# Two-layer hybrid encoder on one core: where a branch's gate products run, how they are kept, and when its decays are read

## The chip, the cores and the metric

The kernel runs on one core of one Trainium2 chip. The metric is device time in microseconds of one execution of the whole program, both layers and both sequences. The engines are TensorE (PE, its weight loads apart as PEld), VectorE (DVE), ScalarE (ACT), GpSimd (POOL) and SyncE (SP), which issues all DMAs of this kernel from one queue.

## The reference, cut to what matters

Two sequences of 256 and 512 tokens (T = 768 together) go through two layers with 1024 channels. `layer` below is one of them; the three branches are a state-space scan (SSD), gated linear attention (GLA) and attention, and each has a sigmoid gate.

```python
h = rmsnorm(x, norm1_w)
z, xbc, dt_raw, gq, gk, gv, gog, glr, aq, ak, av, gates = split(h @ w_in)
# SSD: xbc through a depthwise conv of 5 taps and silu, dt by softplus; chunks of 128 tokens
y = y_forward + y_backward + xs * d_skip
o_ssd = rmsnorm(y * silu(z), norm_w)
o_gla = gla(gq, gk, gv, gog, glr)      # forward and backward, chunks of 64 tokens
o_att = attention(aq, ak, av)
g = sigmoid(gates)                     # three gates of 1024 channels
merged = g[0] * (o_ssd @ w_br_ssd) + g[1] * (o_gla @ w_br_gla) + g[2] * (o_att @ w_br_attn)
x = x + merged @ w_out
x = x + (silu(gate) * up) @ w_ffn_out  # on rmsnorm(x, norm2_w), 2816 hidden channels
```

All inputs and outputs are float32.

## The kernel before

The activations lie transposed: 128 channels on the partitions, the 768 tokens along the free dimension. A float32 product is made from two float32r parts of each side, a rounded one and the rest ("hi" and "lo"): for a block of 128 output channels and 1024 input channels `gemm_a` issues 3 pairs of parts x 8 blocks of channels x 2 halves of the tokens = 48 matmuls of 128x384 into one PSUM tile of 768 columns. There are two such PSUM tiles (`pg`). The short products of the scans (128x256, 128x128, 128x64 columns) are plain float32. A product's weights come in units of four blocks (512 columns, 256 KB): `wunit` loads a unit into one of three raw tiles, ACT writes its rounded part and POOL (DVE in the stages where `lo_eng` is set so) the rest, into five pairs of tiles.

A layer is recorded in this order (`layer`, L782): norm; attention with the first inputs of the GLA between its blocks; `ssd_dt` (step sizes, cumulated decays and the decays' factors of the SSD); the GLA's other inputs (`gla_qk`, `gla_v`) and its output gate `gog`; the GLA, two pairs of heads one after the other, each forward and backward (`gla_pair`), followed by the eight products `g2` and `ba` of the attention's gate and its branch; the SSD in four groups (`ssd_inputs` with four `xbc` products each, `ssd_group`), between which the eight `g1` and `bg` products of the GLA's branch stand; then the loop of the SSD's gated outputs (L869: eight `z` products, silu, times y, split into parts, sum of squares), its norm, the eight `g0` and `bs` products of the SSD's branch; `wo`; and the feed-forward part.

Nothing runs in the recorded order. Every operation is first recorded in a plan; `schedule` then lets the plan run on assumed costs (`cost`; a DMA is taken to land 1900 ns behind its transfer) and hands each engine, whenever it is free, the operation with the lowest number whose inputs and buffers are there. What is recorded under `first` comes before everything else. So operations recorded later fill an engine while an earlier chain waits, if their buffers are free: tiles of one stage share SBUF cells with those of the next. The order so found is written out and fixed: each engine, and SP's queue, does its operations one by one, and waits for what the next one needs. All instructions therefore carry the line of `emit`, L563, and are told apart by their shapes and tiles (`base_S` and `base_P` are the kernel's lasting tiles in SBUF and PSUM, `cell` those of a stage, `wts` the weights, `d_...` tensors kept in DRAM).

Tiles that matter below: `ea` (two, used by every gate and every gated output), `ld` (one, into which y, partial sums and the residual are loaded), `yz` (eight pairs, the split outputs of the SSD).

## Time and profile before

| what | value |
|---|---|
| time, median of 3 runs | 3194.85 us (3192.27 to 3194.99) |
| the profiled execution | 3194.44 us, span 3192.7 us |
| mean granted TensorE clock | 0.98 |
| busy: PE, PEld, DVE, ACT, POOL | 96%, 94%, 50%, 40%, 29% |
| ACT table loads | 149 |
| HBM read, written | 235 MB, 41 MB |

The span is what lies between the first and the last instruction. A busy share is a mean over stages that differ: the feed-forward part (1060 to 1601 us in the first layer) is nothing but matmuls, the scans are chains through PE, DVE, ACT and POOL. The granted clock is 1.00 where TensorE runs at its upper level, 2.4 GHz, and 0.5 at the lower, 1.2 GHz; a mean between them tells what share of a stretch was at which.

### The profile page before, as it was taken

Reading aid. Unit: us, or ns where it says so; the run is one execution under the profiler, and the core shown is the slowest. Engines: PE = TensorE matmul, PEld = TensorE weight load, DVE = VectorE, ACT = ScalarE, POOL = GpSimd, SP = SyncE. Lnnn points to the kernel's source line nnn. Section 1 sums busy time; section 2 is a strip of 40 time slices with the busy share of each in tenths; the row PEclk is TensorE's granted clock in tenths of the full one; section 3 lists DMA queues with packets and bytes.
Section 4 is the critical chain, followed back from the end, with each engine's and each line's share of the span. In section 5 each row is a group of like instructions: output and inputs, shape, how many; then the busy total and the mean of one; then the engine's idle time right before and its main releaser. Section 6 shows DMA issues by size and latency. Waiting matters only on the chain.

```text
span 3192.7 us, 46598 instructions
## 1 busy us (share of the span) xinstructions
PE 3068.3 (96%) x18160; PEld 2997.0 (94%) x18160; DVE 1604.1 (50%) x2777; ACT 1262.3 (40%) x2153; POOL 932.1 (29%) x932
## 2 busy tenths in 40 slices
PE   8989988999999999999999899799999999999998
PEld 7989977899999999999999899599999999999998
DVE  4765578666423332333447556776663234333333
ACT  4667545444323221212346665444443232222123
POOL 4533544554232000000164244355533320000002
PEclk8999988999999999999999999799999999999999
DMA  3223213443334322222222232133443252222222
GB/s 109 60 74 111 92 43 100 124 118 107 98 88 132 115 62 65 62 65 61 90 78 65 74 118 81 38 110 116 117 126 90 86 178 64 63 63 64 63 60 70
DMA packets 191949, 279.31 MB, mean 87 GB/s; under 512 B 16688, under 2 KB 89776, under 8 KB 191728
## 3 DMA queue, kind: packets, MB, share of 16 engines
q1 hardware_dynamic: 191728, 276.32, 29.3%
q8 instruction: 143, 2.34, 0.3%
q14 instruction: 78, 0.64, 0.1%
HBM read 235.17 MB, written 41.09 MB: 87 GB/s over the span
## 4 chain that ended last, share of the span: by engine, by line
PE 86%; DVE 8%; DMA 3%; ACT 2%; issue 1%; POOL 0%; SPq 0%; DVEq 0%; POOLq 0%; ACTq 0%
PE base_P L563 86%; DVE cell L563 7%; DMA cell<-d_cs 2%; ACT cell L563 1%; DVE base_S L563 1%; DMA d_ce<-cell 1%; ACT L563 0%; ACT base_S L563 0%; DMA cell<-d_ce 0%; POOL cell L563 0%; SPq L563 0%; DMA base_S<-wts 0%; DMA cell<-xT 0%; DMA base_S<-d_part 0%; POOL base_S L563 0%
## 5 line engine op out<-in xcount | busy, mean ns | idle before, releaser
L563 PE MATMUL base_P<-base_S 128*128 128x384 f32 (+3 forms) x12452 | 2265.6, 335 | 42.9 <-DVE cell L563 21.2
L563 PEld LDWEIGHTS base_P<-base_S 128*128 128x128 f32 x12452 | 2113.8, 190 | 58.4 <-DVE cell L563 23.6
L563 ACT ACTIVATE base_S<-base_S 128x512 fp32r<-128x512 f32 (+6 forms) x830 | 550.6, 668 | 1299.2 <-PE base_P L563 914.2
L563 DVE TENSOR_TENSOR base_S<-base_S,base_S 128x512 fp32r<-128x512 f32 (+1 forms) x400 | 281.5, 704 | 692.1 <-issue 526.1
L563 PE MATMUL base_P<-cell,base_S 128*128 128x384 f32 x3136 | 574.2, 337 | 0.0
L563 POOL TENSOR_TENSOR cell<-cell,base_S 128x256 f32<-128x256 f32 (+3 forms) x164 | 183.9, 1132 | 1319.0 <-ACT base_S L563 1288.8
L563 PEld LDWEIGHTS base_P<-cell,base_S 128*128 128x128 f32 x3136 | 550.8, 188 | 0.0
L563 POOL TENSOR_TENSOR base_S<-base_S,base_S 128x512 fp32r<-128x512 f32 (+1 forms) x232 | 315.9, 1363 | 449.3 <-ACT base_S L563 192.0
L563 DVE TENSOR_TENSOR base_S<-base_P,base_S 128x768 f32<-128x768 f32 (+1 forms) x276 | 231.5, 839 | 295.5 <-PE base_P L563 284.0
L563 PE MATMUL base_P<-cell,cell 128*128 128x256 f32 (+3 forms) x1568 | 314.7, 325 | 21.8 <-DVE cell L563 16.4
L563 PEld LDWEIGHTS base_P<-cell,cell 128*128 128x128 f32 x1568 | 237.8, 191 | 50.7 <-DVE cell L563 19.4
L563 DVE TENSOR_TENSOR cell<-base_P,cell 64x128 f32<-64x128 f32 (+5 forms) x385 | 201.7, 528 | 155.7 <-PE base_P L563 93.6
L563 ACT ACTIVATE cell<-base_P 128x256 f32<-128x256 f32 (+5 forms) x344 | 148.3, 440 | 177.3 <-PE base_P L563 156.5
L563 POOL TENSOR_TENSOR cell<-cell,cell 128x256 f32<-128x256 f32 (+6 forms) x244 | 179.4, 747 | 95.8 <-DVE cell L563 59.1
L563 PE MATMUL base_P<-base_S,cell 128*128 128x128 f32 (+2 forms) x908 | 161.6, 288 | 39.9 <-ACT cell L563 19.0
L563 ACT ACT_TABLE_LOAD x149 | 191.2, 1283 | 7.9 <-DMA cell<-xT 5.3
L563 ACT ACTIVATE cell<-cell 128x768 f32<-128x768 f32 (+9 forms) x228 | 133.2, 608 | 128.4 <-DVE cell L563 122.0
L563 PEld LDWEIGHTS base_P<-base_S,cell 128*128 128x128 f32 x908 | 116.0, 156 | 63.2 <-ACT cell L563 22.8
L563 DVE SCALAR_TENSOR_TENSOR cell<-cell,base_S,cell 128x770 f32<-128x770 f32 x128 | 150.5, 1175 | 30.9 <-ACT cell L563 27.8
L563 DVE TENSOR_TENSOR cell<-cell,base_S 128x1024 f32<-128x1024 f32 (+3 forms) x85 | 87.4, 1050 | 32.0 <-DMA cell<-d_cs 22.6
L563 POOL TENSOR_TENSOR base_S<-base_S 128x768 f32<-128x768 f32 x32 | 67.0, 2095 | 110.1 <-DVE base_S L563 110.1
L563 DVE TENSOR_TENSOR cell<-base_P,base_S 128x256 f32<-128x256 f32 (+1 forms) x136 | 67.0, 512 | 63.1 <-PE base_P L563 61.2
(58 smaller groups left out, 1194.5 us busy)
## 6 DMA issues: line engine op xcount, KB each, us to landing
base_S<-wts SPq DMA_DIRECT2D x584, 256.0 KB, 2.6
cell<-d_cs SPq DMA_DIRECT2D x96, 256.0 KB, 4.7
d_part<-base_S SPq DMA_DIRECT2D x32, 384.0 KB, 2.8
base_S<-d_part SPq DMA_DIRECT2D x32, 384.0 KB, 3.5
base_S<-wts SPq DMA_DIRECT2D x32, 272.0 KB, 2.7
d_y<-cell SPq DMA_DIRECT2D x48, 128.0 KB, 3.7
base_S<-d_y SPq DMA_DIRECT2D x16, 384.0 KB, 3.4
d_x<-base_S SPq DMA_DIRECT2D x16, 384.0 KB, 2.5
```

What stands on the lines that cost most here:

```text
L563: f(*[real(x) for x in op.args], **{k: real(x) for k, x in op.kw.items()})
```

## The change

- The eight `z` products, with silu, are recorded behind `g2`/`ba` in the GLA's stage; the results go to DRAM (`d_z`), and the loop of gated outputs loads them.
- Six of the eight `g0` products, with sigmoid, are recorded earlier: two behind the SSD's last group, one behind every second gated output; the results go to DRAM (`d_g0`) and are loaded where `gate_branch` used to make them. `g0` 6 and 7 stay.
- The gates `g1` and `g2` are made by tanh, which shares a table with exp in the plan (`SETS`): sigmoid(x) is (1 + tanh(x/2))/2. The half is left to the end: the branch's product is multiplied by 2 for the SSD, and `wo`'s result by 0.5. These factors ride in SCALAR_TENSOR_TENSOR instructions that replace TENSOR_TENSOR ones.
- The tail of `ssd_dt`, which reads the chunk ends' decays back from DRAM (`ce`) and takes their exponentials, becomes `ssd_decays` and is recorded behind `gla_v(1)`.
- The plan's landing time of a DMA is 8400 ns with an element-strided side in SBUF, 4000 ns with a broadcast source, and 1900 ns else.

```diff
-SETS = {"Exp": (0,), "Ln": (5,), "Sigmoid": (2,), "Silu": (18,), "Sqrt": (3,)}
+SETS = {"Exp": (0,), "Tanh": (0,), "Ln": (5,), "Sigmoid": (2,), "Silu": (18,), "Sqrt": (3,)}
...
+    def landing(out, src):
+
+        if any(v.dims[-1][0] > 1 and v.dims[-1][1] not in (0, 1) and v.buf.space == "S" for v in (out, src)):
+            return 8400
+        if any(s == 0 and n > 1 for n, s in src.dims):
+            return 4000
+        return 1900
...
-                        op.end = start + cost + 1900
+                        op.end = start + cost + op.landing
...
         self.gla_v(1)
+        self.ssd_decays()
...
             self.gate_branch("g2", "ba", m, self.o_att, None, self.d_part[m])
+
+        early = [("z", m) for m in range(8)] + [("g0", m) for m in range(6)]
+        for _ in range(8):
+            self.early_gate(*early.pop(0))
...
+            for _ in range((0, 0, 0, 2)[g]):
+                self.early_gate(*early.pop(0))
...
-            ps = self.gemm_in(l, "z", m)
             ea = self.ev.tile([P, T], F32, tag="ea", bufs=2)
-            self.dve.tensor_tensor(out=ea, in0=ps, in1=self.r1, op=ALU.mult)
-            self.act.activation(ea, ea, AF.Silu)
+            self.sp.dma_start(ea, self.d_z[m])
...
+            if m % 2 and early:
+                self.early_gate(*early.pop(0))
+        for g in early:
+            self.early_gate(*g)
...
-            mg.append(self.gate_branch("g0", "bs", m, yz, self.d_part2[m], None, rs))
+            mg.append(self.gate_branch("g0", "bs", m, yz, self.d_part2[m], None, rs, self.d_g0[m] if m < 6 else None))
...
-            self.dve.tensor_tensor(out=x, in0=ps, in1=x, op=ALU.add)
+            self.dve.scalar_tensor_tensor(out=x, in0=ps, scalar=0.5, in1=x, op0=ALU.mult, op1=ALU.add)
...
+    def early_gate(self, name, m):
+        ps = self.gemm_in(self.l, name, m)
         with self.first():
             ea = self.ev.tile([P, T], F32, tag="ea", bufs=2)
             self.dve.tensor_tensor(out=ea, in0=ps, in1=self.r1, op=ALU.mult)
-            self.act.activation(ea, ea, AF.Sigmoid)
+            self.act.activation(ea, ea, AF.Silu if name == "z" else AF.Sigmoid)
+            self.sp.dma_start((self.d_z if name == "z" else self.d_g0)[m], ea)
...
+            if gate is None:
+                self.dve.tensor_tensor(out=ea, in0=ps, in1=self.r1, op=ALU.mult)
+            else:
+                self.sp.dma_start(ea, gate)
+
+            if rs is None:
+                self.act.activation(ea, ea, AF.Tanh, scale=0.5)
+            elif gate is None:
+                self.act.activation(ea, ea, AF.Sigmoid)
...
-            self.dve.tensor_tensor(out=ea, in0=ps2, in1=ea, op=ALU.mult)
+            if rs is None:
+                self.dve.scalar_tensor_tensor(out=ea, in0=ea, scalar=1.0, in1=ps2, op0=ALU.add, op1=ALU.mult)
+            else:
+                self.dve.scalar_tensor_tensor(out=ea, in0=ps2, scalar=2.0, in1=ea, op0=ALU.mult, op1=ALU.mult)
```

What that does to the engines' fixed order is shown at three places of the first layer. In the second layer they look alike. The emitting line is L563 before and L574 now, and the lasting tiles are numbered 83 to 85 before and 87 to 89 now.

**ACT, behind the attention's blocks.** `base_S<-cell 128x192` is the exponential of the chunk ends' decays, which needs `ce` from DRAM; the rows around it are the attention's and the weights' (`128x512`). Before:

```order
L563 ACTIVATE base_S_85<-cell_3_500 128x128
L563 ACTIVATE cell_3_287,cell_3_294<-base_P_84,cell_3_294 128x256
L563 ACTIVATE cell_3_530<-base_P_84 128x256
L563 ACTIVATE base_S_85<-base_S_83 128x512
L563 ACTIVATE base_S_83<-cell_3_550 128x192
L563 ACTIVATE cell_3_550<-base_P_84 64x256
L563 ACTIVATE cell_3_834<-base_P_84 128x512
```

Now:

```order
L574 ACTIVATE cell_3_554<-base_P_88 64x256
L574 ACTIVATE cell_3_507,cell_3_301<-base_P_88,cell_3_301 128x256
L574 ACTIVATE base_S_89<-base_S_87 128x512
L574 ACTIVATE base_S_87<-cell_3_554 128x192
L574 ACTIVATE cell_3_534<-base_P_88 128x256
L574 ACTIVATE base_S_89<-cell_3_1100 128x128
L574 ACTIVATE base_S_87<-base_S_87 128x192
```

The exponential moved 17 instructions back, behind the rows of the attention that used to follow it; on SP's queue the load of `ce` moved behind the next two loads of weights.

**DVE, in the GLA's second pair, backward direction.** Rows with `128x770` are the taps of the SSD's conv, those with `cell_5` tiles belong to the SSD, `base_S<-base_P,base_S 128x768` scales a gate's or output gate's product, `COPY_PREDICATED` and `64x...` rows are the GLA's. Before:

```order
L563 TENSOR_TENSOR cell_5_4027<-base_P_84,base_S_83 128x256
L563 TENSOR_TENSOR cell_5_4027<-base_P_84,base_S_83 128x512
L563 TENSOR_TENSOR cell_4_3089<-cell_4_3089,cell_4_2796 128x768
L563 COPY cell_4_2821<-cell_4_3089 64x6x64
L563 TENSOR_TENSOR cell_4_2863<-cell_4_2796,cell_4_2965 64x768 x2
L563 TENSOR_TENSOR cell_4_3101<-cell_4_3101,cell_4_2798 128x768
L563 SCALAR_TENSOR_TENSOR cell_5_4062<-cell_5_3634,base_S_83,cell_5_4062 128x770 x4
L563 TENSOR_TENSOR cell_5_3634<-base_P_84,base_S_83 128x256
L563 TENSOR_TENSOR cell_5_3634<-base_P_84,base_S_83 128x512
L563 COPY cell_4_2821<-cell_4_3089 64x6x64
L563 SCALAR_TENSOR_TENSOR cell_5_4116<-cell_5_3634,base_S_83,cell_5_4116 128x770 x2
L563 TENSOR_TENSOR cell_4_2821<-cell_4_2821,cell_4_2798 128x768
```

Now:

```order
L574 TENSOR_TENSOR base_S_87<-base_P_88,base_S_87 128x768
L574 SCALAR_TENSOR_TENSOR cell_4_3061<-base_S_87,cell_4_2829 128x64 x3
L574 TENSOR_TENSOR base_S_87<-cell_4_3061 128x6
L574 TENSOR_TENSOR cell_4_3091<-cell_4_3091,cell_4_2795 128x768
L574 TENSOR_TENSOR cell_4_2853<-cell_4_2795,cell_4_2975 64x768 x2
L574 TENSOR_TENSOR base_S_87<-base_P_88,base_S_87 128x768
L574 TENSOR_TENSOR cell_4_3112<-cell_4_3112,cell_4_2797 128x768
L574 COPY cell_4_2810<-cell_4_3091 64x6x64 x2
L574 TENSOR_TENSOR cell_4_2810<-cell_4_2810,cell_4_2797 128x768
```

The `xbc` products of the SSD's first group, which filled TensorE here with their convs behind them, have made room for the `z` products with one scaling each; `xbc` 0 to 3 now stand behind the GLA's last matmul.

**SP, at the loop of the SSD's gated outputs.** `d_y` and `d_z` are the outputs and their gates, `d_g_0` the SSD branch's gates, `wts` units of weights. Before, from the last store of the GLA's branch on:

```order
L563 DMA d_part_0_61<-base_S_83 128x768
L563 DMA base_S_83<-d_y_64 128x768
L563 DMA base_S_83<-wts 128x512 x2
L563 DMA base_S_83<-d_y_64 128x768
L563 DMA base_S_83<-wts 128x512 x2
```

Now, at the loop's end:

```order
L574 DMA base_S_87<-d_z_66 128x768 x2
L574 DMA base_S_87<-wts 128x512
L574 DMA base_S_87<-d_y_64 128x768
L574 DMA base_S_87<-wts 128x512
L574 DMA d_g_0_67<-base_S_87 128x768
L574 DMA base_S_87<-wts 128x512
L574 DMA base_S_87<-d_y_64 128x768
L574 DMA base_S_87<-d_z_66 128x768 x2
L574 DMA base_S_87<-d_y_64 128x768
L574 DMA d_g_0_67<-base_S_87 128x768
```

The loop no longer has a product between two loads of y: it has loads of its own for the gates, and the loads for its last two outputs stand behind units of weights, the last of them the second unit of `bs` 3. On TensorE the six `g0` products stand in one row behind the SSD, then `bs` 0 to 5, then `g0` 6.

## Rows read from the trace of the kernel before

**Rows 1.** The page: busy us, share of the span and instructions of each engine.

```profile
PE 3068.3 (96%) x18160; PEld 2997.0 (94%) x18160; DVE 1604.1 (50%) x2777; ACT 1262.3 (40%) x2153; POOL 932.1 (29%) x932
```

**Rows 2.** Stretches of both layers: length, busy us (x instructions) by engine, granted clock.

```profile
core 0: us, PE busy (x) PEld busy (x) DVE busy (x) ACT busy (x) POOL busy (x), PEclk, DMA share, GB/s
183.00:223.00 40.00, 28.41 (x193) 26.70 (x193) 22.69 (x68) 22.71 (x58) 13.53 (x15) 0.91 0.24 53
293.00:382.00 89.00, 88.52 (x504) 86.86 (x503) 45.01 (x80) 52.31 (x72) 51.15 (x47) 1.00 0.34 104
382.00:494.00 112.00, 90.98 (x467) 78.58 (x466) 80.88 (x176) 56.45 (x121) 44.91 (x62) 0.88 0.17 49
494.00:773.00 279.00, 264.27 (x1570) 253.24 (x1570) 202.40 (x304) 125.11 (x186) 156.13 (x155) 0.98 0.41 115
773.00:840.00 67.00, 67.00 (x385) 67.00 (x385) 35.45 (x38) 28.40 (x38) 13.91 (x7) 1.00 0.38 113
1755.00:1796.00 41.00, 29.00 (x193) 27.03 (x193) 23.21 (x70) 22.39 (x58) 13.44 (x15) 0.88 0.19 51
1955.00:2067.00 112.00, 91.25 (x469) 78.81 (x467) 80.12 (x176) 55.80 (x120) 45.20 (x61) 0.88 0.17 48
2067.00:2346.00 279.00, 265.03 (x1573) 254.02 (x1574) 203.33 (x305) 126.21 (x188) 157.83 (x154) 0.98 0.40 115
```

**Rows 3.** Waits from 183 to 223 us: total, times, longest us.

```profile
ACT base_S L563 <- DMA cell<-d_ce: 9.1, 1, 9.1
...
PE base_P L563 <- ACT cell L563: 8.4, 1, 8.4
...
PE base_P L563 <- DVE cell L563: 3.0, 2, 1.6
```

**Rows 4.** Timeline of SP, then of ACT: start us, us, instruction, idle before.

```profile
189.02 0.56 SPq L563 DMA_DIRECT2D d_ce<-cell  x1
189.68 1.00 SPq L563 DMA_DIRECT2D d_gv<-base_S  x2
197.76 0.32 SPq L563 DMA_DIRECT2D cell<-d_ce  x1
```

```profile
192.95 0.63 ACT L563 ACTIVATE base_S<-base_S 128x512 fp32r<-128x512 f32 x1
202.67 0.54 ACT L563 ACTIVATE base_S<-cell 128x192 f32<-128x192 f32 x1 [9.10 <-DMA cell<-d_ce]
203.24 1.00 ACT L563 ACTIVATE cell<-base_P 64x256 f32<-64x256 f32 x2
...
212.62 0.62 ACT L563 ACTIVATE base_S<-base_S 128x512 fp32r<-128x512 f32 x1
```

**Rows 5.** Groups of PE's matmuls from 382 to 494 us, by shape.

```profile
L563 PE MATMUL base_P<-base_S 128*128 128x384 f32 x251 | 51.6, 356 | 7.2 <-DVE cell L563 5.3 <-ACT base_S L563 1.9
```

**Rows 6.** Timeline of PE where the GLA ends and the SSD begins.

```profile
493.70 1.01 PE L563 MATMUL base_P<-base_S 128*128 128x384 f32 x2 [1.92 <-ACT base_S L563]
500.03 2.29 PE L563 MATMUL base_P<-base_S 128*128 128x384 f32 x6 [5.32 <-DVE cell L563]
```

**Rows 7.** DVE's groups: conv taps from 382 to 494 us; then z's stretch, 773 to 860; then the feed-forward part.

```profile
L563 DVE SCALAR_TENSOR_TENSOR cell<-cell,base_S,cell 128x770 f32<-128x770 f32 x10 | 11.7, 1169 | 3.3 <-ACT cell L563 3.2
```

```profile
L563 DVE TENSOR_TENSOR base_S<-base_S,base_S 128x512 fp32r<-128x512 f32 x20 | 17.9, 895 | 16.5 <-issue 8.9 <-PE base_P L563 7.6
L563 DVE TENSOR_TENSOR base_S<-base_P,base_S 128x768 f32<-128x768 f32 x10 | 9.6, 957 | 13.0 <-PE base_P L563 13.0
L563 DVE SCALAR_TENSOR_TENSOR cell<-base_S,cell 128x768 fp32r<-128x768 f32 x8 | 8.2, 1020 | 11.0 <-ACT cell L563 11.0
L563 DVE TENSOR_TENSOR base_S<-base_S 128x768 f32<-128x768 f32 x8 | 7.7, 959 | 3.1 <-ACT base_S L563 3.1
```

```profile
L563 DVE TENSOR_TENSOR base_S<-base_S,base_S 128x512 fp32r<-128x512 f32 x115 | 79.0, 687 | 214.2 <-issue 172.9 <-PE base_P L563 41.3
```

**Rows 8.** ACT's and POOL's groups in z's stretch, 773 to 860 us.

```profile
L563 ACT ACTIVATE base_S<-base_S 128x512 fp32r<-128x512 f32 x21 | 13.3, 632 | 42.9 <-PE base_P L563 35.1 <-issue 7.4 <-ACT base_S L563 0.4
L563 ACT ACTIVATE cell<-base_S 128x768 fp32r<-128x768 f32 x8 | 7.4, 925 | 0.0
```

```profile
L563 POOL TENSOR_TENSOR cell<-cell,base_S 128x768 f32<-128x768 f32 x7 | 13.6, 1949 | 57.1 <-ACT base_S L563 57.1
```

**Rows 9.** DMA issues from 773 to 1060 us: count, KB each, median us to landing.

```profile
base_S<-d_y SPq DMA_DIRECT2D x8, 384.0 KB, 3.5
...
cell<-d_x SPq DMA_DIRECT2D x8, 384.0 KB, 6.1
```

**Rows 10.** ACT's table loads in the whole program.

```profile
L563 ACT ACT_TABLE_LOAD x149 | 191.2, 1283 | 7.9 <-DMA cell<-xT 5.3
```

**Rows 11.** DVE's SCALAR_TENSOR_TENSOR out of PSUM, whole program.

```profile
L563 DVE SCALAR_TENSOR_TENSOR base_S<-base_P,base_S 128x768 f32<-128x768 f32 x4 | 3.8, 953 | 0.1
```

More of the change, by code (lines that the diff above doesn't have):

```diff
@@ L257 @@
     __slots__ = ("i", "eng", "fn", "args", "kw", "deps", "succ", "cost", "prio", "bufs", "wait", "ready", "end",
-                 "table", "label", "port")
+                 "table", "label", "port", "landing")
 class Proxy:
@@ L349, in record @@
         op.port = eng == "gpsimd" or eng == "vector" and all(v.buf.space == "S" for v in writes + reads)
+        if eng == "sync":
+            op.landing = self.landing(writes[0], reads[0])
         for j in deps:
@@ L380, in cost @@
         return 60 + nbytes / 340
+    @staticmethod
+    def landing(out, src):
[4 more added lines that the diff above has]
+        return 1900
     @staticmethod
@@ L795, in layer @@
         self.d_x = dram("d_x", [8, P, T])
+        self.d_z = dram("d_z", [8, P, T])
+        self.d_g0 = dram("d_g0", [8, P, T])
         self.d_x2 = dram("d_x2", [8, P, T])
@@ L991, in gate_inputs @@
         self.dve.tensor_tensor(out=self.glr[64:128], in0=dtg[64:128], in1=gh[64:128].bitcast(F32), op=ALU.subtract)
-    def gate_branch(self, gname, bname, m, acts, part_in, part_out, rs=None):
-        l = self.l
-        ps = self.gemm_in(l, gname, m)
+    def early_gate(self, name, m):
+        ps = self.gemm_in(self.l, name, m)
         with self.first():
@@ L998, in gate_branch @@
             self.dve.tensor_tensor(out=ea, in0=ps, in1=self.r1, op=ALU.mult)
-            self.act.activation(ea, ea, AF.Sigmoid)
+            self.act.activation(ea, ea, AF.Silu if name == "z" else AF.Sigmoid)
+            self.sp.dma_start((self.d_z if name == "z" else self.d_g0)[m], ea)
+    def gate_branch(self, gname, bname, m, acts, part_in, part_out, rs=None, gate=None):
+        l = self.l
+        ps = self.gemm_in(l, gname, m) if gate is None else None
+        with self.first():
+            ea = self.ev.tile([P, T], F32, tag="ea", bufs=2)
+            if gate is None:
[6 more added lines that the diff above has]
+                self.act.activation(ea, ea, AF.Sigmoid)
             if rs is not None:
@@ L1384, in ssd_dt, with ssd_decays @@
         self.csn = sn[:, :, 64:128].rearrange("p t (d x) -> p t d x", d=2)[:, :, :, 0:16]
+        self.ce = ce
+    def ssd_decays(self):
+        mp, ce = self.mp, self.ce
         self.ecs = self.cp.tile([P, NT, 2, 16], F32, tag="ecs")
```

## The prediction

> **What bounds the kernel now.** I read the page's shares first: PE 96% and PEld 94% of the span [rows 1]. The reader should see that only about 125 us of the span lie outside PE's busy time, and that no product is removed by this change: TensorE gets the same matmuls in another order. What can be won is idle time and time at the lower clock. So I read the stretches next, and count for each what it loses: its idle time plus (1 - granted clock) times its length. In layer 0, with layer 1 behind it [rows 2]:
>
> - attention's end, 183 to 223: 11.6 idle + 3.6 clock = 15.2 (layer 1: 12.0 + 4.9 = 16.9);
> - the GLA's first pair, 293 to 382: 0.5 idle, clock 1.00, nothing to win;
> - its second pair, 382 to 494: 21.0 + 13.4 = 34.4 (20.8 + 13.4 = 34.2);
> - the SSD, 494 to 773: 14.7 + 5.6 = 20.3 (14.0 + 5.6 = 19.6);
> - the `z` products, 773 to 840: 67.0 of 67.0 busy at 1.00, nothing lost, 385 matmuls, so 0.174 us each.
>
> Together 70 us a layer. The z products are thus a dense block that stands where nothing needs filling, and the change carries it to where 34 us are lost. The last two views are the waits and the timelines, which say why PE stands still: in the first stretch ACT waits 9.1 us for `d_ce`, and PE waits 8.4 us for ACT behind it [rows 3].
>
> **Term 1, the decays: +10 us a layer (4 to 12).** The store of `ce` is issued at 189.02, its load at 197.76, and ACT, idle from 193.6, reads it at 202.67 [rows 4]. All 17 rows which now stand ahead of that exponential ran behind it, from 203.24 to 213.24, so they are 10.0 us of work that ACT can start at 193.6. It reaches the exponential near 203.6, when the load, even if it is not issued earlier, has landed (ACT went on at 202.67). The load moved past two loads of weights on SP, each about a microsecond of queue; that eats the margin and no more. PE's 8.4 us behind ACT goes, and with it most of the clock's 3.6: 12.0. PE's 3.0 us behind DVE [rows 3] stays. I take 10. The low end, 4, is for PE finding half of the wait again at the next link of the attention's chain.
>
> **Term 2, the GLA's second pair: +27 (20 to 34).** PE ran 251 matmuls of 384 columns there, the `xbc` 0 to 3 and a part of `g1` [rows 5], by 0.174 us 43.7 us of filling. Its own work is then 112 - 34.4 - 43.7 = 33.9 us at the full clock. In their place come eight z products, 384 x 0.174 = 66.8 us: 33.9 + 66.8 = 100.7. If the GLA's chain keeps its 112 us, 11.3 are lost. It should be shorter: the ten conv taps of 1.169 us leave DVE for the later stage [rows 7], against eight scalings of about 0.957 that come [rows 7]; and the matmuls of the chain itself run at 1.00, not 0.88. With no idle gaps the loss is 0. I take 7: 34.4 - 7 = 27. The ends are 34 (no loss) and 20 (a loss of 14, the chain 3 us longer because ACT's silu and its tables stand in it).
>
> **Term 3, the SSD: +3 (-10 to +8).** The 251 displaced matmuls go here: 279 - 20.3 = 258.7 us of work become 302.4. The SSD's own chain fits in some 270, so PE has more to do than the chain is long, and the filling is there. The two gaps of 1.92 and 5.32 at the border [rows 6] are the first SSD matmuls waiting for convs; now `xbc` 0 to 3 stand densely behind the GLA, which wins these 7.2. But the head start is gone: group 0's convs, 10 taps by 1.169 [rows 7] among them, must run before its first short products, with only `g1` and `bg` as cover; if that gives 4 us back I am at +3. The low end, -10, is a whole conv of a group of 10 to 12 us uncovered; the high end 8 is the border gap with no cost.
>
> By PE's row the stage loses 20.3; the weight loads give another reading. The Trainium skill, "Trainium Kernel Development and Optimization", section "Performance Expectations", calls the busy time of matmuls a bad metric, since they are pipelined, and that of weight loads a good one. By it the stage is 253.2 of 279 busy [rows 2] and loses 25.8, and if that were won the sum would have 5.5 us a layer more (3119 rather than 3130, an estimate from that page's rule and these rows).
>
> **Term 4, the loop of gated outputs and the SSD's branch: -8 (-3 to -20).** The loop used to be covered by z's own 66.8 us. Now six `g0` products cover it: 6 x 48 x 0.174 = 50.1 us from the SSD's end. The loads for the last outputs stand behind units of weights in SP's one queue, the last behind the second unit of `bs` 3. That unit needs a raw tile and a pair of tiles for its parts, which come free only as `g0` 5's weights are released, at about 50.1. With hi, 0.63 [rows 8], and lo, 0.90 [rows 7], y6 is issued near 52 and lands 3.5 us later [rows 9], at 55.5. There is one `ld` tile, so y7 waits for y6's product of 0.96 [rows 7], and lands near 60. Each needs another 0.96, then hi 0.93 [rows 8] and lo 1.02 [rows 7]: the parts are there at 58.4 and 62.9. `bs` 0 starts at 50.1, reaches block 6 after 24 matmuls at 54.3 and waits 4.1; it reaches block 7 another 18 later, 61.5, and waits 1.4. `bs` 2 needs a PSUM tile, which waits for the norm's factor behind the last sum of squares (POOL's additions, 1.949 each [rows 8]): about 2 us. Sum 7.5, taken as 8. If y6 and y7 land earlier, 3 stay. With d_x's 6.1 us for a load [rows 9] in place of 3.5, twice, and a lower clock behind the gap, it is up to 20.
>
> On DVE beside POOL the row shows 895 ns for the weights' lo part in z's stretch, against 687 where DVE works alone in the feed-forward part [rows 7]. I use 895 for the lo part and the rows as they are for the others. The Trainium skill, "SBUF — State Buffer", section "SBUF: two separate sides", says that DVE and GpSimd share a port pair by an exclusive lock, so that a DVE operation with two SBUF inputs and a GpSimd operation that reads SBUF exclude each other for a whole instruction. The trace agrees in sign only: 208 ns more is far from a whole 1949. By that rule the last two steps would lose one POOL addition each, 3.9 us a layer, and the sum would be 3138.
>
> **Edits costed at nothing.** SCALAR_TENSOR_TENSOR out of PSUM takes 953 ns [rows 11], TENSOR_TENSOR 957 [rows 7]: no change. The tables go from 149 loads [rows 10] to 105 in the new order, 44 x 1.283 = 56 us of ACT; ACT is 40% busy [rows 1] and in the stages with gates PE waits for it seldom, so they win nothing beside PE, and cost nothing. Stores and loads of `d_z` and `d_g0` are 28 of 0.39 MB a layer, 11 MB, against a DMA share of 0.17 in the second pair's stretch and 0.41 in the SSD's [rows 2]; PE covers them. Without that cover, 28 landings of 3.5 us would be 98 us a layer.
>
> **Sum.** 10 + 27 + 3 - 8 = 32 us a layer, 64 in both. The profiled execution was 3194.44 with a span of 3192.7, and the median of the runs is 3194.85, 0.4 above, so it is a fair base: 3194.4 - 64 = 3130.
>
> **The rivals.**
>
> *A, the chains are the bound, not PE's filling.* The GLA's chain stays 112 us and takes silu's detours on ACT, and group 0's late start makes the SSD's chain the longest: term 1 is 10, term 2 20, term 3 -10, term 4 -8, so 12 a layer, 3170. For it: in the stretch of 382 to 494 PE waits 7.2 us for DVE and 1.9 for ACT only in the filling's own rows [rows 5], so the filling itself was late. Against it: the first pair, filled with products, has a clock of 1.00 and 88.5 of 89 busy [rows 2].
>
> *B, the SSD gains as well.* With 43.7 us more to choose from, its loss falls from 20.3 to about 5: term 3 is 15 and not 3, term 4 -4. (10 + 27 + 15 - 4) x 2 = 96, so 3098. For it: the stretch loses only 7% now. Against it: what remains idle there may be chains with nothing to overlap.
>
> *C, slower: the loop's tiles.* One `ld`, two `ea` tiles for stores and loads: eight gated outputs of 3.5 landing and about 3.7 of work (product, hi, lo and square: 7.2) and four uses for `g0` of about 4.8 (scaling, gate and a store of 2.9, an estimate from the load's 3.5) make (8 x 7.2 + 4 x 4.8)/2 = 38 us with two tiles, under g0's 50.1. It decides only if the loop's loss goes over 40 us a layer, that is if each use of a tile takes about 17 us. At 6.1 for each load [rows 9] it would be 11 us a layer more, not enough: 3152. Behind 40, slower than 3194.
>
> *D, DVE stands still for POOL's whole addition in the loop's last two steps*: 2 x 1.949 [rows 8] a layer, 3138, within the likeliest one's range; the 208 ns of [rows 7] speak for a small part of it only. It is what the rule of the Trainium skill's "SBUF — State Buffer", told above, would do.
>
> **How the numbers follow.** Likeliest, the four terms: 0.60 (of that 0.10 for D), own range 3105 to 3150. A: 0.20. B: 0.13. C, or that nothing changes: 0.07. The time of the likeliest is 3130. The range is 3092 to 3170: it takes in B and A with the bounds of their terms and leaves out C. A run can be told from no change at about 0.2%, 6 us: faster 0.93, within that 0.03, slower 0.04.
>
> **What would show it.** Term 1: no wait of ACT on `d_ce` in 183 to 223, PE's busy time near 28 in about 30 us. Term 2: 384 more z matmuls there, granted clock 0.95 or above from 382 on, where it was 0.88. Term 3: a stretch of about 300 us between the GLA's last matmul and the SSD's, with `xbc` 0 to 3 without a gap at its head. Term 4: a gap of PE at the first `bs`, behind `d_y` or DVE, of some 6 us, and y6's load issued only when `g0` 5 ends. ACT has 105 table loads. I am wrong if the clock stays below 0.9 in the second pair (A), if PE has gaps over 10 us behind the SSD's convs, or if the gap ahead of `bs` is over 20 us (C).

## The result, and the profile after

The changed kernel takes 3119.19 us (median of four runs, 3117.03 to 3120.53) against 3194.92 in the same session: a ratio of 0.9764, with an interval of 0.9747 to 0.9781. That is 75.7 us less, where 64 were forecast; 3130 was predicted, and 3119 lies inside its own range of 3105 to 3150. The span fell from 3192.7 to 3117.7 us.

The page's busy times, which answer to [rows 1]; the instructions of PE are the same 18160:

```profile
PE 3041.2 (98%) x18160; PEld 2983.5 (96%) x18160; DVE 1606.6 (52%) x2737; ACT 1205.3 (39%) x2109; POOL 992.1 (32%) x972
```

The stretches of the changed kernel between the same products as in [rows 2] (columns as there): the attention's end, the GLA's second pair up to the last `z`, the SSD up to the last `bg`, the six `g0` products, the rest up to the first `wo`; then for the second layer the pair, the SSD and the stretch from the first `bs` to the first `wo`:

```profile
183.00:216.80 33.80, 27.85 (x198) 25.97 (x198) 22.39 (x70) 22.58 (x58) 13.13 (x15) 1.00 0.36 62
376.30:480.50 104.20, 100.84 (x590) 94.83 (x589) 81.95 (x169) 61.62 (x127) 53.76 (x64) 1.00 0.29 92
480.50:792.10 311.60, 306.09 (x1835) 297.01 (x1834) 210.05 (x314) 121.52 (x193) 179.09 (x169) 1.00 0.40 114
792.10:844.00 51.90, 50.35 (x288) 50.03 (x287) 26.31 (x28) 20.56 (x28) 9.95 (x5) 1.00 0.57 185
844.00:939.00 95.00, 89.36 (x506) 88.41 (x507) 37.35 (x40) 29.11 (x40) 49.55 (x25) 0.98 0.45 140
1912.30:2018.00 105.70, 102.52 (x591) 96.66 (x590) 81.86 (x169) 61.69 (x127) 54.02 (x64) 0.98 0.29 91
2018.00:2328.20 310.20, 305.59 (x1834) 296.64 (x1833) 209.89 (x314) 121.28 (x193) 177.78 (x168) 1.00 0.39 114
2380.50:2474.80 94.30, 88.89 (x504) 87.93 (x505) 36.70 (x40) 28.78 (x40) 49.69 (x25) 0.98 0.45 140
```

The granted clock in the second pair is 1.00 (0.98 in the second layer) where it was 0.88, and PE stands still for 3.4 us where it was 21.0. The SSD's stretch is idle for 5.5 us at 1.00, where 14.7 were idle at 0.98. A new loss stands in the last part of a layer: 1.6 + 5.6 us idle. In the kernel before nothing was lost from the first `z` to the first `wo`, 204 us:

```profile
773.00:844.00 71.00, 71.00 (x408) 71.00 (x408) 37.97 (x41) 30.49 (x42) 13.91 (x7) 1.00 0.38 112
844.00:977.00 133.00, 133.00 (x772) 133.00 (x771) 37.11 (x50) 35.32 (x51) 45.21 (x23) 1.00 0.29 85
```

To set these against the four terms, each stretch is taken with the same products in it on both sides (z's 66.8 us and the 43.7 us of displaced matmuls are moved as the prediction moved them). First layer: the pair was 112 + 66.8 - 43.7 = 135.1 and is 104.2; the SSD was 279 + 43.7 = 322.7 and is 311.6; the rest was 204 - 66.8 = 137.2 and is 51.9 + 95.0 = 146.9. The start of the pair came earlier by 5.7 us, 376.3 against 382.0. The second layer is counted in the same way; each term is good to about half a microsecond.

| term, us a layer | forecast | layer 0 | layer 1 |
|---|---|---|---|
| 1, attention and decays | +10 | +5.7 | +5.9 |
| 2, the GLA's second pair | +27 | +30.9 | +29.4 |
| 3, the SSD | +3 | +11.1 | +12.3 |
| 4, gated outputs and `bs` | -8 | -9.7 | -9.4 |
| sum | +32 | +38.0 | +38.2 |

Together that is 76 us, 1 more than the span fell by: between `wo` and the feed-forward part of the first layer the changed kernel is about 1 us longer.

PE's longest waits in the second pair of the kernel before, from the timeline of PE (start, us, instruction, idle time before it), at 424 and 445 us:

```profile
424.06 1.23 PE L563 MATMUL base_P<-cell 128*128 128x128 f32 x4 [4.80 <-DVE cell L563]
...
444.92 7.89 PE L563 MATMUL base_P<-base_S 128*128 128x384 f32 x32 [3.81 <-DVE cell L563]
```

and all waits of PE in the same stage of the changed kernel:

```profile
382.35 0.70 PE L574 MATMUL base_P<-cell,cell 128*128 128x256 f32 x2 [0.27 <-ACT cell L574]
428.97 1.53 PE L574 MATMUL base_P<-cell,cell 128*128 128x256 f32 x6 [2.63 <-DVE cell L574]
447.91 0.71 PE L574 MATMUL base_P<-cell 128*128 128x128 f32 x4 [0.34 <-DVE cell L574]
```

The row at 444.92 of before is a product's matmul, 128x384: the filling itself waited, for DVE to empty a PSUM tile. When the instructions of the trace are laid against the fixed order, `xbc` 0 was emptied into its conv's raw tile at 393.3, but `xbc` 1, finished at 409.6, only at 443.8, `xbc` 2, finished at 419.3, at 456.9, and `xbc` 3 at 499.0. The second raw tile and the conv's `cx` tile belong to the SSD's stage. So both PSUM tiles were full with products that had no place to go, and PE had only the GLA's chain. In the plan the second raw tile lies in the cell of the GLA's `gv`, which the scans at 441.31 read last; `xbc` 1 is emptied right behind them (443.85), and the first conv tap (`128x770`) comes behind both long waits:

```profile
441.31 2.29 DVE L563 TENSOR_TENSOR_SCAN cell<-base_S,cell 128x64 f32<-128x64 f32 x12
443.64 0.17 DVE L563 TENSOR_TENSOR base_S<-cell 128x6 f32<-128x6 f32 x1
443.85 1.02 DVE L563 TENSOR_TENSOR cell<-base_P,base_S 128x256 f32<-128x256 f32 x2
...
451.71 5.10 DVE L563 SCALAR_TENSOR_TENSOR cell<-cell,base_S,cell 128x770 f32<-128x770 f32 x4 [2.34 <-ACT cell L563]
```

By the prediction's count (idle time plus what the clock lacks of 1.00) these 40 us lost 21 of the pair's 34.4:

```profile
420.00:440.00 20.00, 14.71 (x50) 9.91 (x50) 12.68 (x34) 6.51 (x12) 13.25 (x17) 0.66 0.08 24
440.00:460.00 20.00, 14.28 (x66) 13.49 (x67) 16.48 (x30) 10.36 (x14) 8.44 (x9) 0.83 0.05 14
```

Where the tail loses its time, PE's first `bs` matmuls in the changed kernel:

```profile
844.29 4.45 PE L574 MATMUL base_P<-cell,base_S 128*128 128x384 f32 x24 [1.84 <-DVE base_S L574]
852.98 0.62 PE L574 MATMUL base_P<-cell,base_S 128*128 128x384 f32 x2 [4.24 <-ACT cell L574]
854.03 8.40 PE L574 MATMUL base_P<-cell,base_S 128*128 128x384 f32 x38 [0.43 <-DVE cell L574]
```

and SP's queue, where the loop begins (the first row stores the gate of `g0` 0):

```profile
803.06 0.33 SPq L574 DMA_DIRECT2D d_g<-base_S  x1
807.56 0.33 SPq L574 DMA_DIRECT2D base_S<-wts  x1
807.94 0.42 SPq L574 DMA_DIRECT2D base_S<-d_z  x1
```

The SSD's last product ends at 792.1, but the first gate `d_z` is loaded 16 us later. The tiles `ea` are given out in the recorded order, and `g0` 0 and 1 are recorded ahead of the loop: `g0` 1 gets its tile when its product is done, and `z` 0's load stands behind that, though in the plan the other of the two tiles is free before.

### The profile page after: what moved, and what is told of

The parts are those of the page before. It is cut to its first block, busy times and chain, and to the rows that moved or that the text cites. A ratio compares the mean times of both kernels' runs of the same rounds, so it can differ in the third digit from the quotient of the medians.

```text
span 3117.7 us, 46591 instructions
## 1 busy us (share of the span) xinstructions
PE 3041.2 (98%) x18160; PEld 2983.5 (96%) x18160; DVE 1606.6 (52%) x2737; ACT 1205.3 (39%) x2109; POOL 992.1 (32%) x972
## 4 chain that ended last, share of the span: by engine, by line
PE 62%; DVE 3%; ACT 1%; DMA 0%; issue 0%; POOL 0%; DVEq 0%; ACTq 0%; POOLq 0%
PE base_P L574 62%; DVE cell L574 3%; ACT cell L574 1%; DVE base_S L574 0%; DMA base_S<-wts 0%; ACT L574 0%; ACT base_S L574 0%; DMA base_S<-d_z 0%; DMA d_g<-base_S 0%; POOL cell L574 0%; DVEq L1669 0%; POOL base_S L574 0%; DVEq L574 0%; ACTq L574 0%; POOLq L574 0%
## 5 line engine op out<-in xcount | busy, mean ns | idle before, releaser
L574 PE MATMUL base_P<-base_S 128*128 128x384 f32 (+3 forms) x12452 | 2262.1, 334 | 14.0 <-DVE base_S L574 9.6
L574 PEld LDWEIGHTS base_P<-base_S 128*128 128x128 f32 x12452 | 2103.6, 189 | 25.0 <-DVE base_S L574 12.1
L574 ACT ACTIVATE base_S<-base_S 128x512 fp32r<-128x512 f32 (+6 forms) x830 | 549.9, 668 | 1285.6 <-PE base_P L574 862.0
L574 POOL TENSOR_TENSOR cell<-cell,base_S 128x256 f32<-128x256 f32 (+3 forms) x164 | 185.9, 1144 | 1334.1 <-ACT base_S L574 1280.9
L574 PE MATMUL base_P<-cell,base_S 128*128 128x384 f32 x3136 | 577.9, 339 | 14.4 <-ACT cell L574 8.2
L574 DVE TENSOR_TENSOR base_S<-base_S,base_S 128x512 fp32r<-128x512 f32 x360 | 262.9, 730 | 627.1 <-issue 448.2
L574 PEld LDWEIGHTS base_P<-cell,base_S 128*128 128x128 f32 x3136 | 553.1, 189 | 16.9 <-ACT cell L574 8.8
L574 POOL TENSOR_TENSOR base_S<-base_S,base_S 128x512 fp32r<-128x512 f32 (+1 forms) x272 | 369.0, 1359 | 450.0 <-ACT base_S L574 185.2
L574 PE MATMUL base_P<-cell,cell 128*128 128x256 f32 (+3 forms) x1568 | 307.3, 322 | 21.5 <-ACT cell L574 13.3
L574 PEld LDWEIGHTS base_P<-cell,cell 128*128 128x128 f32 x1568 | 238.0, 191 | 45.7 <-ACT cell L574 18.3
L574 DVE TENSOR_TENSOR base_S<-base_P,base_S 128x768 f32<-128x768 f32 (+1 forms) x212 | 170.4, 804 | 212.9 <-PE base_P L574 212.2
L574 DVE TENSOR_TENSOR cell<-base_P,cell 64x128 f32<-64x128 f32 (+5 forms) x385 | 201.8, 527 | 125.4 <-PE base_P L574 85.9
L574 ACT ACTIVATE cell<-base_P 128x256 f32<-128x256 f32 (+5 forms) x344 | 148.1, 441 | 156.9 <-PE base_P L574 143.6
L574 POOL TENSOR_TENSOR cell<-cell,cell 128x256 f32<-128x256 f32 (+6 forms) x244 | 180.5, 753 | 86.2 <-DVE cell L574 49.6
L574 ACT ACTIVATE cell<-cell 128x768 f32<-128x768 f32 (+9 forms) x228 | 132.8, 608 | 145.3 <-DVE cell L574 140.4
L574 PE MATMUL base_P<-base_S,cell 128*128 128x128 f32 (+2 forms) x908 | 153.3, 276 | 15.8 <-DVE cell L574 10.0
L574 DVE SCALAR_TENSOR_TENSOR cell<-cell,base_S,cell 128x770 f32<-128x770 f32 x128 | 140.3, 1096 | 40.4 <-ACT cell L574 36.8
L574 PEld LDWEIGHTS base_P<-base_S,cell 128*128 128x128 f32 x908 | 113.8, 150 | 32.8 <-DVE cell L574 12.4
L574 ACT ACT_TABLE_LOAD x105 | 134.7, 1283 | 8.7 <-DMA cell<-xT 5.2
L574 DVE TENSOR_TENSOR cell<-base_P,base_S 128x256 f32<-128x256 f32 (+1 forms) x136 | 67.2, 512 | 98.8 <-PE base_P L574 97.8
L574 DVE TENSOR_TENSOR cell<-cell,base_S 128x1024 f32<-128x1024 f32 (+3 forms) x85 | 100.2, 1200 | 14.9 <-ACT base_S L574 9.2
L574 DVE TENSOR_TENSOR cell<-cell,cell 128x256 f32<-128x256 f32 (+4 forms) x134 | 92.2, 701 | 24.9 <-ACT cell L574 23.9
```

The source lines that it names most:

```text
L574: f(*[real(x) for x in op.args], **{k: real(x) for k, x in op.kw.items()})
```

## The experiments

Each was run in three rounds with the kernel before on the same chip. What is compared is the ratio to before; a difference of ratios is turned into us by 3195.

**landing_back.** The plan's landing time is 1900 ns for every DMA again.

```diff
-                        op.end = start + cost + op.landing
+                        op.end = start + cost + 1900
```

> The changed kernel with the plan's landing time back at 1900 ns for every DMA; the decays stay recorded late, and the exponential of ce then stands again as the 204th row of ACT in the first layer and not the 221st. Theory (ACT's wait for d_ce is the whole of the term): the wait of about 9 us is back, and since the changed kernel reaches the GLA's stage 5.9 us earlier in either layer, 3119 + 12 = 3131 (3127 to 3135), with nothing changed behind the attention. Rival one, the term as predicted, 10 us a layer: 3139. Rival two, the order of the decays does not matter and the 5.9 us come from tanh's tables: 3119 to 3122.

3139.88 us, ratio 0.9816 (0.9801 to 0.9831), 0.0052 or 16.6 us above the changed kernel: 8.3 a layer, between the theory's 6 and the 10 of the prediction; the two intervals leave some 3.5 us a layer either way. ACT's wait from 183 to 225 us is back:

```profile
ACT base_S L574 <- DMA cell<-d_ce: 10.2, 1, 10.2
```

Its gate products `gog` begin at 209.7 where the changed kernel has 198.7, and the second pair at 385.0 where that has 376.3; from there on the distance stays, 9.4 at `wo`. The other half of this edit changes nothing: with `ssd_decays` recorded in its old place and the new landing times the fixed order of every engine is row for row that of the changed kernel. The landing times alone made term 1.

**decays_alone.** The kernel before with the landing times and the later decays, as in the diff ahead of the prediction, and nothing else of it.

> The kernel before with the plan's new landing times and the decays recorded later, nothing else. Theory (the term stands by itself, 8.3 us a layer as the landing time taken back showed): 3195 - 17 = 3178 (3174 to 3182). Rival one, what the traces of before and after differ by at the second stage, 5.9 a layer: 3183. Rival two, the GLA's second pair, still with its own waits, eats what is won ahead of it: 3190 to 3195.

3176.68 us, ratio 0.9942 (0.9927 to 0.9956), 18.5 us less: 9.3 a layer, as the theory says. It comes in two parts. The pair begins 6.4 us earlier (375.6 against 382.1), a little more than the 5.7 of the changed kernel; the rest is won behind its start, as the new landing times move other rows too:

```profile
183.00:197.00 14.00, 11.84 (x96) 11.41 (x97) 9.90 (x30) 9.41 (x26) 5.76 (x7) 1.00 0.41 38
375.50:482.00 106.50, 88.77 (x465) 76.69 (x464) 77.91 (x172) 55.02 (x119) 45.18 (x61) 0.92 0.17 50
```

The pair still idles for 17.7 us at 0.92: the decays and landing times do not cure it.

**sigmoid.** The gates `g1` and `g2` by sigmoid again, without the factors.

```diff
-            self.dve.scalar_tensor_tensor(out=x, in0=ps, scalar=0.5, in1=x, op0=ALU.mult, op1=ALU.add)
+            self.dve.tensor_tensor(out=x, in0=ps, in1=x, op=ALU.add)
...
-            if rs is None:
-                self.act.activation(ea, ea, AF.Tanh, scale=0.5)
-            elif gate is None:
+            if gate is None:
                 self.act.activation(ea, ea, AF.Sigmoid)
...
-            if rs is None:
-                self.dve.scalar_tensor_tensor(out=ea, in0=ea, scalar=1.0, in1=ps2, op0=ALU.add, op1=ALU.mult)
-            else:
-                self.dve.scalar_tensor_tensor(out=ea, in0=ps2, scalar=2.0, in1=ea, op0=ALU.mult, op1=ALU.mult)
+            self.dve.tensor_tensor(out=ea, in0=ps2, in1=ea, op=ALU.mult)
```

> The changed kernel with sigmoid for g1 and g2 and the factors 2 and 0.5 taken out again: 159 table loads in place of 105. Theory (ACT's tables lie beside PE's products): 3119, 3115 to 3125. Rival: 54 loads of 1.283 us are 69 us of ACT, and half of them on the chains of the GLA and the SSD would give 3150; then the clock in the second pair falls below 1.00 again.

3122.6 us, ratio 0.9759 (0.9743 to 0.9776): the same as the changed kernel's 0.9764. The pair and the SSD take 102.6 and 311.8 us. With 140 us of work in the SSD's stretch in place of 121.5, PE stands still for 1.7 and 5.1 us, where the changed kernel has 3.4 and 5.5:

```profile
377.00:479.60 102.60, 100.92 (x592) 95.32 (x591) 74.17 (x168) 65.90 (x128) 51.79 (x66) 1.00 0.31 92
479.60:791.40 311.80, 306.73 (x1834) 296.09 (x1833) 213.81 (x317) 140.06 (x208) 181.90 (x171) 1.00 0.41 114
```

**narrow_taps.** The kernel before, with the convs of the SSD's first group cut to 128 columns. The other columns of those convs are left out of the computation.

```diff
+                n = CW if g else 128
-                self.dve.scalar_tensor_tensor(out=acc, in0=raw[:, k:k + CW], scalar=self.prm(C_CW + 5 * m + k),
-                                               in1=acc, op0=ALU.mult, op1=ALU.add)
+                self.dve.scalar_tensor_tensor(out=acc[:, 0:n], in0=raw[:, k:k + n], scalar=self.prm(C_CW + 5 * m + k),
+                                               in1=acc[:, 0:n], op0=ALU.mult, op1=ALU.add)
```

> The kernel before, with the conv taps of the SSD's first group cut to 128 of their 770 columns (the other columns of that conv are left out): DVE loses some ten taps of 1.169 us from the GLA's second pair and six from the border, matmuls stay. Theory of the prediction (the taps on DVE hold the GLA's chain and the filling up): the pair's loss of 34.4 falls by about 10 and the border's gap of 5.3 goes, 12 to 15 us a layer: 3195 - 27 = 3168 (3162 to 3176). Rival (what was missing is enough filling that waits for nothing, not DVE's time): 0 to 4 a layer, 3187 to 3195, the clock in the second pair stays near 0.88.

3173.16 us, ratio 0.9928 (0.9912 to 0.9945): 23 us less, 11.5 a layer, a little under the theory's 12 to 15 and far from the rival's 0 to 4. The edit takes about half of the taps' time away (598 ns on the mean where [rows 7] has 1169). But the two long waits in the middle of the pair stand as before:

```profile
425.37 1.22 PE L563 MATMUL base_P<-cell 128*128 128x128 f32 x4 [4.81 <-DVE cell L563]
...
446.01 7.27 PE L563 MATMUL base_P<-base_S 128*128 128x384 f32 x32 [3.87 <-DVE cell L563]
...
488.85 4.21 PE L563 MATMUL base_P<-base_S 128*128 128x384 f32 x12 [2.47 <-DVE cell L563]
```

The taps cost what lies at the pair's end and at the border (5.32 in [rows 6], 2.47 here), where a raw tile is held until they are done with it; the 4.8 and 3.9 are not DVE's time in the taps. That leaves 42 - 11.5, some 30 us of what the pair and the SSD won, that this run doesn't explain; what the taps' other half is worth stays open.

**z_six.** Six `z` products behind the GLA's branch, two behind groups 1 and 2 of the SSD.

```diff
-        for _ in range(8):
+        for _ in range(6):
             self.early_gate(*early.pop(0))
...
-            for _ in range((0, 0, 0, 2)[g]):
+            for _ in range((0, 1, 1, 2)[g]):
```

> The changed kernel with six z products behind the GLA's branch and the other two behind the SSD's groups 1 and 2. The two products, 16.7 us, leave the second pair, and xbc products with their convs may move into it again. Theory (amount and kind of the filling set the pair's loss): a quarter of the 31 us a layer is given back, 3119 + 16 = 3135 (3127 to 3142). Rival (the stage is as long as its matmuls, and the SSD takes the two products at the same price): 3116 to 3123, the second pair shorter by 16 us and the SSD longer by as much.

3122.37 us, ratio 0.9773 (0.9759 to 0.9788): the same as the changed kernel, so the rival. With 50 us of z in place of 67 the GLA's part still runs at the full clock, is shorter by the matmuls taken out, and hands over without a gap at 462, when `xbc` 0 starts:

```profile
375.80:470.00 94.20, 90.86 (x532) 84.91 (x531) 73.29 (x160) 53.66 (x116) 45.42 (x60) 1.00 0.28 87
470.00:480.00 10.00, 10.00 (x60) 10.00 (x59) 9.81 (x14) 6.33 (x8) 4.24 (x4) 1.00 0.35 107
```

How many `z` products fill the pair does not matter between six and eight: at its end `xbc` 0 can follow, finished at 472.0 and emptied at 472.4. That the filling's tiles matter, and not its amount, fits this run; the run does not show it by itself.

**g0_in_place.** All eight `g0` products ahead of their `bs`, `z` early.

```diff
-        early = [("z", m) for m in range(8)] + [("g0", m) for m in range(6)]
+        early = [("z", m) for m in range(8)]
...
-            for _ in range((0, 0, 0, 2)[g]):
-                self.early_gate(*early.pop(0))
...
-            if m % 2 and early:
-                self.early_gate(*early.pop(0))
...
-            mg.append(self.gate_branch("g0", "bs", m, yz, self.d_part2[m], None, rs, self.d_g0[m] if m < 6 else None))
+            mg.append(self.gate_branch("g0", "bs", m, yz, self.d_part2[m], None, rs))
```

> The changed kernel with all eight g0 products in their old place, ahead of their bs; z stays early. The loop of gated outputs then has only g0 0 beside it (8.4 us). Theory of the prediction (7.2 us for an output, two ea tiles): the loop takes about 29 us and 6 behind it, so 27 a layer are open against 9.4 in the changed kernel: 3119 + 35 = 3154. Rival one: an output takes 6 to 8 us one by one, as the loads of y follow each other in the changed kernel, some 56 a layer, 48 open: 3196, all that z won. Rival two: the SSD's last group covers most outputs: 3110 to 3125.

3157.78 us, ratio 0.9873 (0.9859 to 0.9888): 0.0109 or 35 us above the changed kernel, as forecast. Without cover the loop leaves PE 16.8 of 51.9 us idle and at a clock of 0.70. From the SSD's end to `wo` it takes 165.4 us, 28 over the 137.2 of before, where 27 had been worked out:

```profile
793.10:845.00 51.90, 35.10 (x153) 28.56 (x152) 25.30 (x25) 20.70 (x26) 15.56 (x8) 0.70 0.53 157
845.00:958.50 113.50, 112.33 (x643) 112.01 (x643) 33.28 (x43) 28.83 (x41) 43.23 (x22) 1.00 0.31 85
```

**loop_first.** No `g0` behind the SSD's last group; the six stand behind outputs 1 to 6.

```diff
-            for _ in range((0, 0, 0, 2)[g]):
-                self.early_gate(*early.pop(0))
...
-            if m % 2 and early:
+            if 1 <= m <= 6:
                 self.early_gate(*early.pop(0))
```

> The changed kernel with no g0 behind the SSD's last group: g0 0 is recorded behind the second gated output, and one more behind each that follows, so that the two ea tiles go to z 0 and z 1 first. Theory (the tiles are the cause): in the changed kernel z 0 could be loaded only when g0 0's gate was stored, 16 us behind the SSD's end; now the loop starts at once, y 7 is there before bs 0 begins, and the tail loses 1 to 3 us a layer in place of 9.4: 3119 - 14 = 3105 (3101 to 3109). Rival, the prediction's: the last loads stand behind units of weights on SP, whose tiles come free with g0 5, whatever came before: 3116 to 3120.

3104.12 us (3101.74 to 3105.10), ratio 0.9704 (0.9689 to 0.9718): 0.0060 or 19 us below the changed kernel, whose interval it does not touch. The theory holds: the time is within its 3101 to 3109. SP's rows at the loop's head (the first `d_z` comes ahead of the SSD's last matmuls, which end at 791.0 here), then PE's at the first `bs`:

```profile
784.86 0.46 SPq L574 DMA_DIRECT2D base_S<-d_z  x1
...
794.76 0.42 SPq L574 DMA_DIRECT2D base_S<-d_y  x1
796.98 0.32 SPq L574 DMA_DIRECT2D base_S<-d_z  x1
...
842.00 0.32 SPq L574 DMA_DIRECT2D base_S<-d_y  x1
```

```profile
834.68 6.66 PE L574 MATMUL base_P<-base_S 128*128 128x384 f32 x37
841.18 8.03 PE L574 MATMUL base_P<-cell,base_S 128*128 128x384 f32 x45
850.00 3.23 PE L574 MATMUL base_P<-cell,base_S 128*128 128x384 f32 x17 [0.79 <-ACT cell L574]
```

The last y is loaded at 842.00, behind the start of the first `bs` and not ahead of it as the theory had it, but in time: that `bs` has no wait ahead of it, and 0.79 us is what is left of the 1.84, 4.24 and 0.43. From the first `g0` to `wo` it takes 929.5 - 790.8 = 138.7 us, 1.5 over the 137.2 of before. This is the fastest of all kernels here.

## Why the prediction was right, and where it was not

The likeliest case came about: one large gain in the second pair, a small one ahead of it, and a loss in the tail. The total came nearer than its terms, and that is in part luck: term 1 was 4 us a layer too high, term 2 some 3 and term 3 some 8 to 9 too low. Term by term:

**Term 1** forecast +10 and came out at 5.7 and 5.9 between the two kernels, 8.3 when taken back and 9.3 alone, with what is won in the pair: right in mechanism, some 4 too high against the change itself. The wait for `d_ce` is gone from 183 to 216.8, as the 17 rows' cover said, with a clock of 1.00. What the sum left out is the next wait behind it. ACT now waits 2.0 us at 200.60 for `d_gv<-base_S`, a store that must leave its tile first, and PE stands still behind it:

```profile
203.38 0.50 PE L574 MATMUL base_P<-cell,cell 128*128 128x256 f32 x2 [2.72 <-ACT cell L574]
```

In the kernel before, the same store landed inside the 9.1 us. The later place of the decays moves no row by itself; the landing times do.

**Term 2** forecast +27 and came out at 30.9 and 29.4. The working (34.4 lost, 100.7 us of work in what was 112) fits the 104.2 measured. The reason beside it was half of the truth. Half of the taps' time on DVE is worth 11.5 a layer in the pair and the border together (narrow_taps). But 21 of the 34.4 us were lost from 420 to 460, most of it ahead of the first tap at 451.71: the `xbc` products need the SSD's tiles, so the filling stood in PSUM; z's results go to `ea`, a lasting tile, and to DRAM. That this blocking is the cause was read from the trace and the plan and fits narrow_taps (long waits unchanged) and z_six (less filling, same time); no kernel was run that gives the `xbc` products tiles of their own, so it is not shown by a run.

**Term 3** was the mis-sized one: +3 forecast, +11.1 and +12.3 measured, beyond its end of +8. Two steps failed. It counted the border as the two gaps of 1.92 and 5.32 and left out the clock behind them; 20.3 had been read with 5.6 of clock in it, and in the kernel before that clock was low at just this place (0.53 from 491 to 505, 1.00 from 505 to 560):

```profile
491.00:505.00 14.00, 6.66 (x24) 5.66 (x25) 13.73 (x16) 5.34 (x7) 4.31 (x2) 0.53 0.14 37
505.00:560.00 55.00, 54.07 (x323) 52.29 (x322) 45.08 (x65) 27.64 (x39) 32.42 (x32) 1.00 0.44 125
```

And it charged 4 us for the first group's late start, which cost nothing: `g1` and `bg` covered it, 49.00 of 49.50 us busy behind the border:

```profile
480.50:530.00 49.50, 49.00 (x291) 47.72 (x289) 26.59 (x37) 19.64 (x30) 21.91 (x23) 1.00 0.24 71
```

With 5.3 of gap and 5.6 of clock the term would have been 10.9. The other gap, 1.92, was counted twice: it ends at 493.70, inside the pair's stretch, and the matmuls behind it are `bg`'s, which wait for the GLA's result and not for a conv.

Rival B had the size of this term (15) nearly right, with its tail of -4 too mild; rival A did not appear, the pair being as long as its matmuls.

**Term 4** forecast -8 and came out at -9.7 and -9.4, with waits of 1.84, 4.24 and 0.43 at `bs` where 4.1, 1.4 and 2 had been worked out. The place and the size were right and the cause was wrong, so the size is in part luck. The prediction let the last loads wait for units of weights that come free with `g0` 5. In loop_first `g0` 5 ends as late behind the SSD as in the changed kernel, and all but 1.5 us of the loss goes when the loop gets its first tiles at once. The count of tile uses in rival C had left out `g0` 0 and 1, which stand ahead of the loop in the order of `ea` and shift it by 16 us.

**Costed at nothing**, and so it was: the tables (sigmoid: 54 loads more, no time), and SCALAR_TENSOR_TENSOR out of PSUM, now 955 ns where [rows 11] has 953.

**Rival D**, DVE standing still for POOL's whole addition, did happen, at a smaller price than its 3.9 us a layer. The lo parts of the loop's stretch take 929 ns on the mean, near the 895 of [rows 7], but the mean mixes two kinds: 0.68 us where POOL is idle, and up to 2.35 where an addition runs. POOL's row, then DVE's:

```profile
840.86 1.96 POOL L574 TENSOR_TENSOR cell<-cell,base_S 128x768 f32<-128x768 f32 x1 [4.63 <-ACT base_S L574]
```

```profile
841.02 2.35 DVE L574 TENSOR_TENSOR base_S<-base_S,base_S 128x512 fp32r<-128x512 f32 x1
843.29 0.94 DVE L574 TENSOR_TENSOR base_S<-base_P,base_S 128x768 f32<-128x768 f32 x1
844.16 0.68 DVE L574 TENSOR_TENSOR base_S<-base_S,base_S 128x512 fp32r<-128x512 f32 x1
```

The lo part begins inside the addition and ends 0.55 us behind it. The row at 843.29 empties the PSUM tile of `g0` 4, and PE's wait of 1.84 at 844.29 ends with it; the 2.35 - 0.68 = 1.7 us (an estimate; no run takes POOL's additions away) are thus in the tail's loss. The prediction read 208 ns more as a small part of a stop; it is whole stops of a few instructions, spread over all. The rule of the Trainium skill's "SBUF — State Buffer", section "SBUF: two separate sides", an exclusive lock for a whole instruction, is what this trace shows.

The reading by weight loads, under which the SSD lost 25.8 and not 20.3, gives 14.6 after (311.6 - 297.01): 11.2 won. By PE's own row 20.3 became 5.5: 14.8. The lengths say 11.1, so the sentence of the Trainium skill's "Trainium Kernel Development and Optimization", section "Performance Expectations", that busy time of weight loads is the better measure, held here for the gain. That its estimate of the time, 3119, is the measured one is luck: by it term 3 would have been 8.5, and the other terms make up the rest.

## What to carry to other kernels

As the trace reads here, filling for a stalled stage is worth its matmuls only if its result has a place to go: ask of each filling product which tile it is emptied into and who holds that tile, before counting microseconds. When a dense block is moved away, count what it covered; the loop behind it needed other cover, worth 35 us over both layers, and the order in which shared tiles are given out decided whether that cover was whole. An idle gap is priced with the clock behind it, and behind a long wait that is removed the next one is already standing. A mean over a group of instructions can hide a few that stand still: look at single rows before calling a stop small.

## What the hardware showed

- The clock came back where the gaps went. In the changed kernel's second pair one long gap of 2.63 us goes with a granted clock of 1.00 in the first layer and 0.98 in the second; with gaps of 4.80 and 3.81 that stage had 0.88.
- The table loads cost ACT's time and nothing else: 105 loads in place of 149 are 134.7 us in place of 191.2 [rows 10], and with 159 the program was as fast.
- A DVE instruction with two inputs in SBUF that begins while POOL runs a TENSOR_TENSOR of its own ends behind it. In the trace of before, 366 of the 384 lo parts on DVE (128x512) begin with none running and take 0.69 us, 0.70 at most; the other 18 all end 0.55 to 0.60 us behind POOL's instruction, and the longest takes 1.40. So it is with two conv taps ahead of the gap of 5.32 in [rows 6]: they take 2.39 and 2.44 us, where taps beside an idle POOL take 1.02, as POOL runs two instructions of its own from 493.80 to 498.11. DVE's emptying of a PSUM tile is not held: at 854.08 of the changed kernel it takes 0.96 us beside an addition that runs from 853.74 to 855.67.
- In loop_first, at 207 GB/s from 790 to 841 us, the loads of `d_z` and `d_y` take 3.9 and 4.0 us at the median, where `d_y` took 3.5 in the kernel before [rows 9], beside 113 GB/s from 773 to 840 [rows 2]. But in the changed kernel, at 185 GB/s, `d_y` takes 3.4 and `d_z` 3.7, so the load on the queues alone is not shown to be the reason.
